# Decoder trunk on one core: weight loads by contraction halves in the ConvFFN's first two blocks, a large PSUM tile for their last product, another distribution of the adaLN sections, and merge tiles fetched ahead

## The chip, the cores and the metric

The kernel runs on one core of a Trainium2 chip, in one launch. The metric is the device time of the program in microseconds. The kernel before was run three times; its time is the median.

## The reference, cut to what matters

A residual trunk of two layers works on x (1024 tokens, 1024 channels, float32) and a conditioning vector c. Layer 0 has the even mixer (gated DeltaNet heads and pooling), layer 1 the odd mixer (dilated attention in three groups, merged per head). Behind each mixer stands a ConvFFN with 2816 hidden channels. In front of each of these four stands a norm with shift and scale from c, and a gate from c stands behind it.

```python
cs = jax.nn.silu(c)
for i in range(DEPTH):
    mod = (cs @ ada_w[i] + ada_b[i])[:, None, :]
    sh_m, sc_m, g_m, sh_f, sc_f, g_f = jnp.split(mod, 6, axis=-1)
    hm = rms_norm(x, norm_mix[i]) * (1.0 + sc_m) + sh_m
    ...
    x = x + g_m * y
    hf = rms_norm(x, norm_ffn[i]) * (1.0 + sc_f) + sh_f
    x = x + g_f * conv_ffn(hf, ffn_w_up[i], ffn_conv_w[i], ffn_conv_b[i], ffn_w_down[i])

def conv_ffn(h, w_up, conv_w, conv_b, w_down):
    up = h @ w_up
    gate, val = jnp.split(up, 2, axis=-1)
    gate = causal_dwconv(gate, conv_w) + conv_b
    return (jax.nn.silu(gate) * val) @ w_down
```

In the odd mixer each of the three attention groups gives an output and the logarithm of its softmax denominator per token and head; the outputs are added with weights that are the softmax of the three logarithms.

## The kernel before

**Layout and arithmetic.** Activations lie channel-major: eight tiles of 128 channels by 1024 tokens; a half is 512 tokens. A float32 product is made of three matmuls (`mm3`, L205 to L209): both operands are split into a high and a low part, and high by high, high by low and low by high are accumulated in PSUM. A product of one 128-column block with one half of the activations takes eight steps k of three matmuls each.

**Weights.** `granule` (L186 to L193) loads 128 x 512 floats into one of four raw buffers (`raw`), copies the high part on ScalarE into one of nine `whi` buffers and lets GpSimd subtract to get the low part into one of nine `wlo` buffers (`split`, L182). `unit_c` (L195) loads one column block of 128 output channels as two granules, contraction blocks k = 0 to 3 and k = 4 to 7. All loads are issued by SyncE.

**PSUM.** There are two large tiles (`mm_ps`, 128 x 1024) and four small ones (`s_ps`, 128 x 512). A tile that is asked for takes a buffer when its last reader has finished.

**Order.** The text of the program gives each instruction its rank. The tile framework places the buffers and decides the order on each engine; an instruction whose operands and buffer are there can be issued ahead of older ones. `weave` and `mix` set how the text of a chain of small steps is interleaved with a generator of dense products.

**Stages.** Even mixer (to about 510 us), its last projection woven with the next norm (`edge`), ConvFFN of layer 0 (about 554 to 1250), odd mixer (to about 2375), ConvFFN of layer 1, output.

**ConvFFN.** `first_two` (L1147 to L1169) computes channel blocks 0 and 1 directly: gate0 and val0 in the two large tiles, the first halves of gate1 and val1 in two small ones. For the first half of the tokens the four products run side by side, k by k (`units`, L212), interleaved with the norm of the second half; then gate0, val0, gate1 and val1 follow for the second half, one after the other (the last two in new small tiles). The projection ahead of it, `edge`, holds eight granules: four rows of weights, two granules each; it passes over the output blocks once for each half of the tokens. `conv_half` (L1118) does the depthwise convolution on ScalarE and VectorE, `act` (L1128) the silu and the product with val. From block 2 on, `up` (L1240) computes the two halves with seven products in place of eight (a11, a12, s2, s1, s3, s4, a22, four steps each), for which `h_sums` and `w_sums` form sums of activations and weights on VectorE. The products alternate between large and small PSUM tiles. Then the down stage (L1284 to L1288) applies pairs of hidden blocks, nine pairs, with `update` (L222): for each pair 16 output pieces (o, half), 2 x 3 matmuls each.

**adaLN sections.** `mod` is needed in 24 sections of 512 columns, 12 a layer. The first four are done at the start. The rest are generators (`ada_steps`, L259): a section is ten steps, namely the first load, eight multiply-adds (each with the load of the next 256 KB into a raw buffer), and a sum over partitions by TensorE transposes. The multiply-add is one VectorE instruction (L281) or, when `by_pool` is set, a ScalarE multiplication and a GpSimd addition (L275, L277). There are two accumulators. `step_back` is called once by every product step (L218), by `update` and by `up`; every `pace`-th call gives out one step, as long as fewer than `secs_due` sections are done. `sections(n)` gives out what is missing up to n at once. Before: pace 3 up to section 12 in the even mixer; pace 14 with 24 due in the up stage of layer 0, by VectorE; pace 2 in its down stage, by ScalarE and GpSimd, and the rest at its end.

**Merges.** After the attention of a head pair, `merge` (L1576) reads for each of eight token blocks the three groups' outputs (three DMAs of 128 x 2 x 130 floats into one of three `ld` buffers), forms the weights and adds; `turn_o` transposes the result. The DMAs of a block stand in the text right ahead of the instructions that read them.

Of the kernel before, what the change touches and what calls it, by code (L numbers as in the profile page):

```python
# [34 lines left out]
def trunk(ctx, tc, x, c, ada_w, ada_b, norm_mix, norm_ffn, ev_w_in, ev_w_out, gdn_conv_w,  # L35
# [69 lines left out]
    pa = [None]  # L105
    back = []
    by_pool = [False]
    beat, pace, secs_done, secs_due = [0], [3], [0], [12]

    def step_back(now=False):  # L110

# [75 lines left out]
    def granule(src, shape=None):  # L187
# [4 lines left out]
        split(hi, lo, raw, lo_eng[0])  # L192
        return hi, lo  # L193

    def unit_c(w, c0):  # L195

        blocks = []
        for g in range(0, KT, 4):
            hi, lo = granule(w[g * P:(g + 4) * P, c0:c0 + P].rearrange("(k p) c -> p k c", p=P),
                             ("p (k c) -> p k c", dict(k=4)))  # L200
            blocks += list(zip(blk4(hi), blk4(lo)))
        return blocks

    def mm3(ps, wb, mov, first, last):

# [244 lines left out]
    def even():  # L450
# [9 lines left out]
        with tc.tile_pool(name="pe", bufs=1) as pe:  # L460
# [266 lines left out]
            def dense():  # L727
# [9 lines left out]
                ready.add(("in", 0))  # L737
                back.append(ada_steps(0, range(16, 48, 4), raw_tile))
                back.append(ada_steps(1, range(0, 48, 4), raw_tile))
                with tc.issue_after(res["gt"].ins):  # L740
                    step_back(True)
                    step_back(True)
# [344 lines left out]
            drain(dn)  # L1087
            xt = res["x"]
            h2 = h_tiles()
            sections(12)  # L1090
            vec2 = norm_vec(0, 1)
            acc = edge(row_blocks(ev_w_out[0], (6, 7, 2, 3)), [*res["o67"], res[2], res[3]], gate, xt, vec2, h2, xs[2])
            return xt, h2, vec2, acc
# [2 lines left out]
    def ffn(l, xt, h, vec, acc, vec_next):  # L1096
        gate = mod[l][:, 40:48]
        wu, wd = ffn_w_up[l], ffn_w_down[l]
        with tc.tile_pool(name=f"pf{l}", bufs=1) as pf:
# [38 lines left out]
            def ext(dt=F32R, name="ext"):  # L1138
                return pf.tile([P, T], dt, tag="ext", name=nm(name), bufs=8)

            def wu_gate(j):
                return unit_c(wu, j * P)

            def wu_val(j):
                return unit_c(wu, DFF + j * P)

            def first_two():  # L1147

                gp, vp = mm_ps(), mm_ps()
                g, v = ([[p[:, s] for s in HS], [s_ps(), None]] for p in (gp, vp))  # L1150
                wb = [wu_gate(0), wu_val(0), wu_gate(1), wu_val(1)]
                t = [gate_tile(), gate_tile()]
                d = units([gp, vp, g[1], v[1]], wb, h, (0,))
                weave(norm(xt, vec, h, 1, acc, (4.5, 6.0), keep=True), d)
                drain(d)
                drain(units([gp], wb[:1], h, (1,)))
                for hf in range(2):
                    conv_half(t[0], g[0], 0, hf)
                conv_half(t[1], g[1], 1, 0)
                drain(units([vp], wb[1:2], h, (1,)))  # L1160
                act(t[0], v[0], 0)
                sums = h_sums()
                g[1][1] = s_ps()
                drain(units([[None, g[1][1]]], wb[2:3], h, (1,)))
                conv_half(t[1], g[1], 1, 1)
                v[1][1] = s_ps()
                drain(units([[None, v[1][1]]], wb[3:], h, (1,)))
                act(t[1], v[1], 1)
                return sums  # L1169
# [98 lines left out]
            sums = first_two()  # L1268
            a = w_sums(2)
            if l == 0:  # L1270
                secs_due[0], pace[0] = 24, 14
                with tc.issue_after(last_act[0].ins):
                    step_back(True)
                    step_back(True)
# [5 lines left out]
                up(j, b, a)  # L1280
                a = nxt
            xt = reload(xs[2 + l])
            pace[0], by_pool[0] = 2, True
            for j in range(0, NJ - 4, 2):  # L1284
                if j:
                    hid = [from_dram(hid_d[l][i]) for i in (j, j + 1)]
# [12 lines left out]
    def odd(xt, h, vec, acc):  # L1299
# [5 lines left out]
        with tc.tile_pool(name="po", bufs=1) as po:  # L1305
# [274 lines left out]
            def merge(hp, need):  # L1580
# [5 lines left out]
                elif hp == 3:  # L1586
                    o = [et("qkT", 4, (P, 2, T), F32R) for _ in range(2)]
                    o = [(t[:, 0, :], t[:, 1, :]) for t in o]
                    res["m3"] = [halves(*t) for t in o]
                mos = {}  # L1590

                def load(t):
                    ld = et("ld", 3, (P, 3, 2, 130))
                    for g in range(3):
                        nc.sync.dma_start(ld[:, g], osc[g][t * P:(t + 1) * P, hp * 2:hp * 2 + 2, :])
                    mx, e, dn = et("mx", 2, (P, 1, 2)), et("me", 2, (P, 3, 2)), et("dn", 2, (P, 3, 2))
                    nc.vector.tensor_reduce(out=mx[:, 0, :], in_=ld[:, :, :, 128].rearrange("p g x -> p x g"),
                                            axis=mybir.AxisListType.X, op=ALU.max)
                    nc.vector.tensor_tensor(out=e, in0=ld[:, :, :, 128], in1=mx.to_broadcast([P, 3, 2]), op=ALU.subtract)
                    nc.scalar.activation(e, e, AF.Exp)  # L1600
                    nc.vector.tensor_tensor(out=dn, in0=e, in1=ld[:, :, :, 129], op=ALU.mult)
                    nc.vector.tensor_reduce(out=mx[:, 0, :], in_=dn.rearrange("p g x -> p x g"),
                                            axis=mybir.AxisListType.X, op=ALU.add)
                    nc.vector.reciprocal(mx, mx)
                    nc.vector.tensor_tensor(out=e, in0=e, in1=mx.to_broadcast([P, 3, 2]), op=ALU.mult)
                    if t % 2 == 0:
                        mos[t // 2] = t2k()
                    for hh in range(2):
                        m = blk4(mos[t // 2])[hh * 2 + t % 2]
                        nc.scalar.activation(m, ld[:, 0, hh, 0:P], AF.Copy, scale=e[:, 0, hh:hh + 1])  # L1610
                        for g in (1, 2):
                            nc.vector.scalar_tensor_tensor(out=m, in0=ld[:, g, hh, 0:P], scalar=e[:, g, hh:hh + 1],
                                                           in1=m, op0=ALU.mult, op1=ALU.add)
# [127 lines left out]
```

## Time and profile before

| what | value |
|---|---|
| median of three runs | 3058.81 us (3058.46 to 3065.91) |
| the profiled execution | 3069.38 us, of which the span is 3067.3 us |
| mean granted TensorE clock in the span | 0.983 |
| HBM read / written | 251.82 / 77.00 MB |
| DMA packets of SyncE's and ScalarE's queue (q1) | 300.55 MB, 31.2% of 16 engines |

How to read it: PE is TensorE's matmuls, PEld its weight loads, DVE is VectorE, ACT ScalarE, POOL GpSimd, SP SyncE, whose DMA issues are not counted as busy. L207 is line 207 of the kernel. In a group, "sp<-hh,whi" is a matmul that writes a small PSUM tile from activations hh with weights whi; "mm" is a large one. "[1.65 <-ACT whi L184]" says that the engine was idle for 1.65 us before the instruction, and that the idle time ended with ScalarE's writing of whi on line 184. "x40: 733/752/1885" are 40 instructions with the shortest, the median and the longest duration in ns. Durations of matmuls overlap.

### The profile page before, as it was taken

Reading aid. Unit: us, or ns where it says so; the run is one execution under the profiler, and the core shown is the slowest. Engines: PE = TensorE matmul, PEld = TensorE weight load, DVE = VectorE, ACT = ScalarE, POOL = GpSimd, SP = SyncE. Lnnn points to the kernel's source line nnn. Section 1 sums busy time; section 2 is a strip of 40 time slices with the busy share of each in tenths; the row PEclk is TensorE's granted clock in tenths of the full one; section 3 lists DMA queues with packets and bytes.
Section 4 is the critical chain, followed back from the end, with each engine's and each line's share of the span. In section 5 each row is a group of like instructions: output and inputs, shape, how many; then the busy total and the mean of one; then the engine's idle time right before and its main releaser. Section 6 shows DMA issues by size and latency. Waiting matters only on the chain.

```text
span 3067.3 us, 40298 instructions
## 1 busy us (share of the span) xinstructions
PE 2965.9 (97%) x14346; PEld 2452.8 (80%) x14346; DVE 1945.1 (63%) x3781; ACT 1138.9 (37%) x2266; POOL 1033.0 (34%) x783
## 2 busy tenths in 40 slices
PE   6999999899999999999999999999999999999999
PEld 4777877778888887888888878888877788888888
DVE  6768745987776655654545646353687877776554
ACT  5433432533334433423333434333344433334210
POOL 4412323565556876200000010000032555556540
PEclk8999999999999999999999999999999999999999
DMA  7523314253323754322214242313253222224321
GB/s 247 142 61 107 96 59 151 72 155 110 110 86 102 237 156 138 129 67 73 92 62 123 72 145 74 106 41 113 65 175 117 73 89 83 83 83 168 110 91 58
DMA packets 275011, 331.47 MB, mean 108 GB/s; under 512 B 27411, under 2 KB 194426, under 8 KB 274810
## 3 DMA queue, kind: packets, MB, share of 16 engines
q1 hardware_dynamic: 266810, 300.55, 31.2%
q0 software_dynamic: 7040, 25.17, 2.4%
q10 hardware_dynamic: 960, 3.18, 0.3%
q8 instruction: 113, 1.85, 0.3%
q14 instruction: 88, 0.72, 0.1%
HBM read 251.82 MB, written 77.00 MB: 107 GB/s over the span
## 4 chain that ended last, share of the span: by engine, by line
PE 73%; DVE 6%; POOL 2%; issue 2%; DMA 2%; ACT 1%; SPq 0%; POOLq 0%; ACTq 0%; DVEq 0%
PE sp L209 11%; PE sp L207 11%; PE sp L208 11%; PE mm L1365 8%; PE mm L1363 8%; PE mm L1364 8%; PE mm L208 3%; PE mm L207 3%; PE mm L209 3%; PE sp L1559 2%; PE sp L1515 2%; PE sp L1395 1%; DVE xr L1181 1%; PE sp L1548 1%; POOL wlo L185 1%
## 5 line engine op out<-in xcount | busy, mean ns | idle before, releaser
L1363 PE MATMUL mm<-whi,hh 128*128 128x512 f32 x1152 | 482.6, 419 | 0.0
L1365 PE MATMUL mm<-whi,hl 128*128 128x512 f32 x1152 | 452.7, 393 | 0.0
L1364 PE MATMUL mm<-wlo,hh 128*128 128x512 f32 x1152 | 451.2, 392 | 0.0
L185 POOL TENSOR_TENSOR wlo<-raw,whi 128x512 fp32r<-128x512 f32 x190 | 250.0, 1331 | 492.6 <-ACT whi L184 425.0
L241 DVE SCALAR_TENSOR_TENSOR xr<-sp,mod,xr 128x512 f32<-128x512 f32 x336 | 251.1, 749 | 183.5 <-PE sp L209 183.5
L207 PE MATMUL sp<-oh,whi 128*128 128x512 f32 (+1 forms) x832 | 314.0, 377 | 1.6 <-ACT whi L184 1.6
L184 ACT ACTIVATE whi<-raw 128x512 fp32r<-128x512 f32 x334 | 207.9, 629 | 286.9 <-PE sp L208 100.9
L209 PE MATMUL sp<-oh,wlo 128*128 128x512 f32 (+1 forms) x832 | 311.7, 375 | 2.2 <-POOL wlo L185 1.9
L208 PE MATMUL sp<-ol,whi 128*128 128x512 f32 (+1 forms) x832 | 311.1, 374 | 0.0
L207 PE MATMUL mm<-hh,whi 128*128 128x512 f32 x704 | 285.3, 405 | 1.7 <-DVE big L609 1.7
L208 PE MATMUL mm<-hl,whi 128*128 128x512 f32 x704 | 280.0, 398 | 2.2 <-DVE hl L385 2.2
L185 POOL TENSOR_TENSOR wlo<-t2k,whi 128x512 fp32r<-128x512 f32 x160 | 228.3, 1440 | 156.2 <-ACT whi L184 96.8
L209 PE MATMUL mm<-hh,wlo 128*128 128x512 f32 x704 | 279.8, 397 | 0.0
L1460 POOL DMA_DIRECT2D vd<-v x24 | 17.6, 735 | 771.6 <-ACT v L1457 380.7
L1365 PEld LDWEIGHTS mm<-whi,hl 128*128 128x128 f32 x1152 | 216.4, 188 | 47.8
L1364 PEld LDWEIGHTS mm<-wlo,hh 128*128 128x128 f32 x1152 | 217.8, 189 | 37.0
L1363 PEld LDWEIGHTS mm<-whi,hh 128*128 128x128 f32 x1152 | 217.4, 189 | 36.0
L185 POOL TENSOR_TENSOR wlo<-wr,whi 128x512 fp32r<-128x512 f32 x114 | 179.2, 1574 | 159.5 <-ACT whi L184 151.4
L209 PEld LDWEIGHTS sp<-oh,wlo 128*128 128x128 f32 x832 | 157.2, 189 | 31.9 <-POOL wlo L185 4.2
L207 PEld LDWEIGHTS sp<-oh,whi 128*128 128x128 f32 x832 | 157.4, 189 | 29.8 <-ACT whi L184 2.5
L208 PEld LDWEIGHTS sp<-ol,whi 128*128 128x128 f32 x832 | 157.4, 189 | 26.9
L207 PE MATMUL sp<-hh,whi 128*128 128x512 f32 x384 | 152.3, 396 | 13.5 <-DVE ft L1107 10.2
(401 smaller groups left out, 6238.3 us busy)
## 6 DMA issues: line engine op xcount, KB each, us to landing
raw<-in_ada_w_dram SPq DMA_DIRECT2D x160, 256.0 KB
wr<-in_ffn_w_up_dram SPq DMA_DIRECT2D x76, 512.0 KB
raw<-in_od_w_in_dram SPq DMA_DIRECT2D x144, 256.0 KB
hid<-ft SPq DMA_DIRECT2D x44, 512.0 KB
raw<-in_ffn_w_down_dram SPq DMA_DIRECT2D x88, 256.0 KB
big<-hid SPq DMA_DIRECT2D x44, 512.0 KB
xr<-xs SPq DMA_DIRECT2D x32, 512.0 KB
os<-stg SPq DMA_DIRECT2D x96, 130.0 KB
```

The costliest lines, as they stand in the source:

```text
L184: nc.scalar.activation(dst_hi, src, AF.Copy)
L185: eng.tensor_tensor(out=dst_lo, in0=src, in1=dst_hi, op=ALU.subtract)
L207: nc.tensor.matmul(ps, wh, mh, start=first, stop=False)
L208: nc.tensor.matmul(ps, wh, ml, start=False, stop=False)
L209: nc.tensor.matmul(ps, wl, mh, start=False, stop=last)
L241: nc.vector.scalar_tensor_tensor(out=xt[o][:, s], in0=p, scalar=gate[:, o:o + 1], in1=xt[o][:, s], op0=ALU.mult, op1=ALU.add)
L1181: nc.vector.tensor_tensor(out=out, in0=x, in1=y, op=ALU.subtract)
L1363: nc.tensor.matmul(p, hh, wh, start=(k == 0), stop=False)
L1364: nc.tensor.matmul(p, hh, wl, start=False, stop=False)
L1365: nc.tensor.matmul(p, hl, wh, start=False, stop=(k == KT - 1))
L1515: nc.tensor.matmul(ps[:, at:at + len(ks) * P], qks[i][0][:, hh, blk * P:(blk + 1) * P], qks[i][1][:, hh, ks[0] * P:(blk + 1) * P], start=T ...
L1559: nc.tensor.matmul(ps[:, j * P:(j + 1) * P], pTs[n][:, a0 + c * P:a0 + (c + 1) * P], vb(kb, hh), start=(c == 0), stop=(c == len(ks) - 1))
```

## The change

1. `units_c` loads several column blocks by contraction halves: first the granule k = 0 to 3 of each column, then k = 4 to 7 of each. `first_two` uses it for its four columns. Before, each column was loaded whole, one after the other.
2. The last product of `first_two` (val1, second half) takes one half of a large PSUM tile instead of a small tile.
3. Sections: the even mixer does sections up to 10 at pace 4 (before: up to 12 at pace 3); the up stage of layer 0 up to 12 at pace 20 (before: up to 24 at pace 14); the down stage of layer 0 the other twelve, at pace 1, by ScalarE and GpSimd (before: what was left, at pace 2).
4. `merge` issues the DMAs of blocks t, t+1 and t+2 ahead of the work on block t.

```diff
-    beat, pace, secs_done, secs_due = [0], [3], [0], [12]
+    beat, pace, secs_done, secs_due = [0], [4], [0], [4]
...
+    def units_c(w, cols_):
+        blocks = [[] for _ in cols_]
+        for g in range(0, KT, 4):
+            for c0, b in zip(cols_, blocks):
+                hi, lo = granule(w[g * P:(g + 4) * P, c0:c0 + P].rearrange("(k p) c -> p k c", p=P),
+                                 ("p (k c) -> p k c", dict(k=4)))
+                b += list(zip(blk4(hi), blk4(lo)))
+        return blocks
+
     def unit_c(w, c0):
-        blocks = []
-        for g in range(0, KT, 4):
-            hi, lo = granule(w[g * P:(g + 4) * P, c0:c0 + P].rearrange("(k p) c -> p k c", p=P),
-                             ("p (k c) -> p k c", dict(k=4)))
-            blocks += list(zip(blk4(hi), blk4(lo)))
-        return blocks
+        return units_c(w, (c0,))[0]
...
                 back.append(ada_steps(1, range(0, 48, 4), raw_tile))
+                secs_due[0], pace[0] = 10, 4
...
-            sections(12)
+            sections(10)
             vec2 = norm_vec(0, 1)
...
-                wb = [wu_gate(0), wu_val(0), wu_gate(1), wu_val(1)]
+                wb = units_c(wu, (0, DFF, P, DFF + P))
...
-                v[1][1] = s_ps()
+                v[1][1] = mm_ps()[:, HS[0]]
                 drain(units([[None, v[1][1]]], wb[3:], h, (1,)))
...
             if l == 0:
-                secs_due[0], pace[0] = 24, 14
+                secs_due[0], pace[0] = 12, 20
...
             xt = reload(xs[2 + l])
-            pace[0], by_pool[0] = 2, True
+            if l == 0:
+                sections(12)
+                secs_due[0], pace[0], by_pool[0] = 24, 1, True
...
-                mos = {}
+                mos, lds = {}, {}
+
+                def fetch(t):
+                    lds[t] = et("ld", 3, (P, 3, 2, 130))
+                    for g in range(3):
+                        nc.sync.dma_start(lds[t][:, g], osc[g][t * P:(t + 1) * P, hp * 2:hp * 2 + 2, :])
 
                 def load(t):
-                    ld = et("ld", 3, (P, 3, 2, 130))
-                    for g in range(3):
-                        nc.sync.dma_start(ld[:, g], osc[g][t * P:(t + 1) * P, hp * 2:hp * 2 + 2, :])
+                    for t_ in range(t, min(t + 3, TT)):
+                        if t_ not in lds:
+                            fetch(t_)
+                    ld = lds[t]
```

More of the change, by code (lines that the diff above doesn't have):

```diff
@@ L1139, in ext @@
                 return pf.tile([P, T], dt, tag="ext", name=nm(name), bufs=8)
[L1141 to L1145, printed above, removed]
             def first_two():
```

## The prediction

> **What bounds the kernel now.** I read the page first, then the waits of TensorE, then its timeline around the longest of them, and last the windows of single stretches.
>
> ```profile
> span 3067.3 us, 40298 instructions
> ...
> PE 2965.9 (97%) x14346; PEld 2452.8 (80%) x14346; DVE 1945.1 (63%) x3781; ACT 1138.9 (37%) x2266; POOL 1033.0 (34%) x783
> ```
>
> TensorE is idle for 3067.3 - 2965.9 = 101 us; none of its matmuls is removed by the change, so the gain lies in those 101 us and in what follows an idle stretch. The profiled execution took 3069.4 us (the span and 2.1 us around it), 10.6 us above the median of 3058.8 of the runs. I make the sum as a difference against the profiled execution and carry the difference over to the median.
>
> In the waits of TensorE (total us, times, longest) two are of the kind that the change names:
>
> ```profile
> PE sp L207 <- DVE ft L1107: 10.2, 2, 6.5
> ...
> PE sp L1395 <- DVE t2k L1381: 5.4, 1, 5.4
> ```
>
> The first stands once in each ConvFFN, at the end of the first two channel blocks; the second is in a merge. The start of each ConvFFN has a pair of its own, here on TensorE's timeline (start, us, instruction, idle before it and its releaser), layer 0 and then layer 1:
>
> ```profile
> 558.50 0.50 PE L207 MATMUL sp<-hh,whi 128*128 128x512 f32 x1 [1.65 <-ACT whi L184]
> ...
> 561.98 0.79 PE L209 MATMUL sp<-hh,wlo 128*128 128x512 f32 x1 [2.52 <-POOL wlo L185]
> ...
> 2375.20 0.50 PE L207 MATMUL sp<-hh,whi 128*128 128x512 f32 x1 [1.64 <-ACT whi L184]
> ...
> 2378.68 0.80 PE L209 MATMUL sp<-hh,wlo 128*128 128x512 f32 x1 [2.52 <-POOL wlo L185]
> ```
>
> An idle stretch has a second price. In the windows below (stretch, its length, PE busy, PEld, DVE, ACT, POOL, granted clock, DMA share, GB/s) the clock is 0.50:
>
> ```profile
> 560.70:567.50 6.80, 5.52 (x15) 4.44 (x16) 3.87 (x3) 1.21 (x2) 4.61 (x4) 0.50 0.37 116
> 611.90:622.10 10.20, 5.85 (x14) 4.62 (x15) 10.20 (x14) 3.77 (x6) 6.39 (x5) 0.50 0.46 145
> 2376.60:2383.40 6.80, 4.71 (x13) 3.74 (x14) 3.57 (x3) 1.85 (x3) 5.41 (x4) 0.50 0.40 124
> ...
> 1205.80:1212.60 6.80, 5.63 (x13) 3.97 (x13) 1.64 (x3) 2.52 (x4) 3.39 (x3) 0.50 0.71 216
> ```
>
> Each lies at or right behind a wait. At half clock, half of the busy time is lost.
>
> **Weights by contraction halves: -13.4.** Before, the four columns are loaded one after the other, two granules each, so the first matmul of val1 (the fourth product at k=0) needs the seventh of eight granules. There are nine buffers for split weights; the projection ahead holds eight, four of which come free halfway through its second pass and four at its very end. The seventh granule is among the late ones: that is the pair of waits above. After the change the first matmuls need granules one to four, all in buffers that are free early. The second halves are needed at k=4, four times four products later. What goes: 1.65 + 2.52 and half of 5.52 = 6.9 in layer 0; 1.64 + 2.52 and half of 4.71 = 6.5 in layer 1. No instruction is added. What is late next would be the norm of the second half, but it shifts along, because VectorE waits there for TensorE:
>
> ```profile
> 567.08 0.69 DVE L313 TENSOR_REDUCE rs<-sp 128x4 f32<-128x512 f32 x1 [2.92 <-PE sp L312]
> ```
>
> The Trainium skill (TensorE: Matmul & The Clock Gate, "What's actually happening") has the clock halved after an idle window of about 3.4 us; the waits here are 1.65 and 2.52 us with matmuls between, and the windows still show 0.50, so the trace does not bear that threshold out for broken idle time. By the page the two half-clock terms would not belong to these waits and the part would bring 8.3.
>
> **The last small tile becomes a large one: -4, between -8.3 and +1.7.** There are four small PSUM tiles and two large ones. Now the last product (val1, second half) takes the fourth small one, and the second product of channel block 2 (a12) finds none: the 10.2 us of the wait above. Layer 0, in order of time:
>
> ```profile
> 601.44 0.39 PE L207 MATMUL sp<-hh,whi 128*128 128x512 f32 x1
> ...
> 604.90 0.20 DVE L1107 SCALAR_TENSOR_TENSOR ft<-mm,cols,ft 128x2 f32<-128x2 f32 x1
> ...
> 606.88 0.39 PE L207 MATMUL mm<-hh,whi 128*128 128x512 f32 x1
> ...
> 610.02 1.27 DVE L1132 TENSOR_TENSOR ft<-ft,mm 128x512 f32<-128x512 f32 x2
> ...
> 616.25 0.77 PE L207 MATMUL sp<-hh,whi 128*128 128x512 f32 x1 [6.49 <-DVE ft L1107]
> ...
> 621.51 0.63 PE L207 MATMUL sp<-ext,whi 128*128 128x512 f32 x1
> ```
>
> At 601.44 the last product starts, at 606.88 a11 (large), at 616.25 a12, at 621.51 the third product. Eight steps of three matmuls take 5.44 us, one 0.68. The change does not remove the scarcity, it moves it: the last product now needs gate0's large tile, free at 604.90 + 0.20 = 605.1 (a new wait of 3.7), and ends at 610.5; a11 then needs val0's large tile, free at 611.3, and ends at 614.0; a12 has a small tile at once and ends at 616.7. That is 4.8 earlier than 621.51. If the new wait halves the clock for 6.8 us, 3.4 of it are lost again. If a12 is put ahead of the last product, the third product waits for the small tile of 616.25: 5.3 earlier. Layer 1:
>
> ```profile
> 2417.79 0.39 PE L207 MATMUL sp<-hh,whi 128*128 128x512 f32 x1
> ...
> 2421.25 0.21 DVE L1107 SCALAR_TENSOR_TENSOR ft<-mm,cols,ft 128x2 f32<-128x2 f32 x1
> ...
> 2426.96 1.27 DVE L1132 TENSOR_TENSOR ft<-ft,mm 128x512 f32<-128x512 f32 x2
> ...
> 2429.83 0.47 PE L207 MATMUL sp<-hh,whi 128*128 128x512 f32 x1 [3.72 <-DVE ft L1107]
> ...
> 2433.92 0.63 PE L207 MATMUL sp<-ext,whi 128*128 128x512 f32 x1
> ```
>
> The same steps: tile free at 2421.5, end 2426.9, val0's tile 2428.2, a11 to 2431.0, a12 to 2433.7: 0.2 earlier, 3.1 later at half clock, 3.0 earlier with a12 put ahead. The sums are -5.0 as written, +1.7 with both half-clock stretches, -8.3 at best; I take -4, near the first. Behind the waiting product on TensorE stands all of block 2; VectorE waits only for val1's multiplication.
>
> **Sections dealt out anew: +1.** Of the 20 sections behind the first four, the even mixer did 8, now 6; the up stage of layer 0 did 4, now 2; the down stage did 8, now 12, by ScalarE and GpSimd.
>
> Even mixer, -2: two sections are 16 VectorE instructions of the row below, 12 us, fewer; and the others come later. Waits of TensorE there, on VectorE:
>
> ```profile
> L281 DVE SCALAR_TENSOR_TENSOR ada_acc<-raw,cs,ada_acc x56: 733/752/1885, 105.5 to 347.3; 128x512 f32<-128x512 f32 x56
> ```
> ```profile
> 148.79 1.11 PE L919 MATMUL sp<-ident,qkv 128*128 128x128 f32 x4 [3.70 <-DVE g L906]
> ...
> 168.98 1.09 PE L937 MATMUL sp<-ident,g 128*128 128x128 f32 x4 [3.47 <-DVE g L929]
> ```
>
> Both fall into the section steps' time. They are chains of a head's small instructions, of which section steps are only a part, so I take -2, between -7.2 (both go) and +3.7 (a section lands in another chain).
>
> Up stage, 0: TensorE was the bound (100 of 100 us busy):
>
> ```profile
> 700.00:800.00 100.00, 100.00 (x447) 82.84 (x446) 77.10 (x92) 35.61 (x51) 56.12 (x38) 1.00 0.33 106
> ```
>
> Down stage, +3. GpSimd's groups in 1000 to 1200 (busy, mean ns), then windows, then the waits at its end:
>
> ```profile
> L277 POOL TENSOR_TENSOR ada_acc<-ada_acc,raw 128x512 f32<-128x512 f32 x49 | 63.6, 1299 | 20.0 <-ACT ada_acc L275 12.0 <-ACT raw L275 6.1 <-POOL ada_acc L277 0.2
> L185 POOL TENSOR_TENSOR ol<-big,oh 128x1024 fp32r<-128x1024 f32 x20 | 48.0, 2401 | 12.7 <-ACT oh L184 12.5
> L185 POOL TENSOR_TENSOR wlo<-raw,whi 128x512 fp32r<-128x512 f32 x33 | 42.2, 1293 | 17.0 <-ACT whi L184 17.0
> ```
> ```profile
> 1000.00:1050.00 50.00, 50.00 (x225) 41.39 (x223) 30.81 (x43) 24.29 (x32) 40.96 (x27) 1.00 0.77 251
> ...
> 1014.00:1164.00 150.00, 150.00 (x675) 124.22 (x674) 87.67 (x120) 62.54 (x85) 119.73 (x81) 1.00 0.60 182
> ```
> ```profile
> 1202.88 0.50 PE L209 MATMUL sp<-oh,wlo 128*128 128x512 f32 x1 [1.22 <-POOL wlo L185]
> 1203.92 0.50 PE L207 MATMUL sp<-oh,whi 128*128 128x512 f32 x1 [0.54 <-ACT whi L184]
> 1205.34 0.50 PE L209 MATMUL sp<-oh,wlo 128*128 128x512 f32 x1 [0.69 <-POOL wlo L185]
> 1206.88 0.80 PE L207 MATMUL sp<-oh,whi 128*128 128x512 f32 x1 [1.04 <-ACT whi L184]
> ```
>
> A beat (one output block of one half, two products) is 2 x 0.68 = 1.36 us. With pace 1 a section of ten steps is due every 13.6 us, all twelve by beat 120 of 144. Two sections can be done ahead in the up stage (two accumulators), a third starts when the first is transposed, at about 1014. So from 1014 to beat 120 at 1163 GpSimd has ten sections of seven additions, 10 x 7 x 1.299 = 90.9, and the weights and hidden tiles of six pairs, 6 x (4 x 1.293 + 2 x 2.401) = 59.8: 151 us of work in 149, where it was busy for 119.7 before. It is full, but the last sections are not needed before the odd mixer's end and can slip into the last 24 beats. DMA: four sections more are 32 x 256 KB in 196 us, 43 GB/s on top of 182; the first row carried 251 without a wait. The load of one step stands on SyncE's queue among those of weights and hidden tiles, and all raw buffers (four) are released by GpSimd; a late section holds the next pair's weights back, and TensorE waits for those. Bounds: -6.3 if the sections end early and the four waits (3.5) with their half clock (half of 5.63) go; +34 if GpSimd can't exceed the 41.0/50 = 82% of the first row, 151/0.82 = 184 us. I take +3: the waits at the end stay and some are added.
>
> **Merges: 0, between -5.4 and +5.4.** Three buffers hold the fetched tiles, before and after. The instructions of an engine aren't issued in the order of the text here, and the fetches already run ahead:
>
> ```profile
> L1595 SPq DMA_DIRECT2D ld<-os x96: 319/424/822, 1415.4 to 2313.5; - x96
> ...
> L1597 DVE TENSOR_REDUCE mx<-ld x32: 147/162/165, 1672.0 to 2318.5; 128x2 f32<-128x6 f32 x32
> ```
>
> The first fetch is issued 257 us before the first read. A fetch waits for a buffer, and that isn't changed; the wait of 5.4 on L1395 bounds it either way.
>
> **Sum.** -13.4 - 4 - 2 + 0 + 3 + 0 = -16.4: 3053.0 for the profiled execution, 3042.4 against the median.
>
> **The rivals.** (1) GpSimd becomes the bound of layer 0's down stage: +34 in place of +3, 3042.4 + 31 = 3073. For it: 151 in 149, and 82% as the densest seen. Against: at 82% TensorE never waited, so it wasn't pushed. It decides from the point where the stage's loss exceeds the other terms' 19.4, which is 151/(149 + 19.4) = 90% of GpSimd's time. The Trainium skill (GPSIMD Engine Reference, "Engine selection") keeps element-wise additions off GpSimd, as about twice as slow as VectorE for two inputs; here it is 1299 against 752 ns, 1.7 times. (2) The gaps fill up again: of the first part only the plain waits go (8.3), the last small tile is even, the down stage costs 3: -5, 3053. For it: VectorE is busy for all of 611.90 to 622.10, so an earlier TensorE may meet the same late instructions. The case that the granules aren't issued in the new order, so that the first part does nothing, gives 3056 and belongs here. (3) All ends of the good side but the merges': -13.4 - 8.3 - 7.2 - 6.3 = -35, 3024.
>
> **How the numbers follow.** A measurement of this kernel can tell about 0.3%, 9.2 us: 3049.6 and 3068.0 are the edges. Forecast 0.49 (3030 to 3049), rival 1 0.15, rival 2 0.23, rival 3 0.13. Faster 0.49 + 0.13 = 0.62, same 0.23, slower 0.15. The range takes in the forecast, rival 2 and most of rival 3, and stops short of rival 1: 3022 to 3066.
>
> **What would show it.** Right: no wait of TensorE on whi and wlo at the start of either ConvFFN and clock 1.00 there; a wait of 3 to 4 us on L1107 moved to the last product of the first two blocks, or gone; GpSimd over 90% busy from 1014 to 1163; merges as before. Wrong: the pair of waits still there or as long further on, at k=4; waits of TensorE on wlo of over 19 us in the down stage; a merge that gains over 5.

## The result and the profile after

The changed kernel takes 3095.6 us (median of 4 runs, 3092.3 to 3097.8) against 3058.6 (4 runs, 3057.0 to 3065.9): ratio 1.0118, 95% interval 1.0105 to 1.0130. It is slower by 37 us, where 16 less were forecast. The spans of the profiled executions differ by 28.8 us (3096.1 and 3067.3); the one of before was 10.6 above its own median, and where these 10.6 lay turns out to matter below.

The stretches of the two traces, cut at the first matmul of each stage on TensorE's timeline:

| stretch (us) | before | after | difference |
|---|---|---|---|
| up to the first product of layer 0's ConvFFN | 554.7 | 550.9 | -3.7 |
| its first two channel blocks, to the third product of block 2 | 66.9 | 56.3 | -10.6 |
| the rest of the up stage | 378.4 | 380.6 | +2.2 |
| layer 0's down stage, to the odd mixer's first product | 253.0 | 296.8 | +43.9 |
| odd mixer, to the first product of layer 1's ConvFFN | 1118.5 | 1122.4 | +3.9 |
| first two blocks of layer 1 | 62.6 | 57.0 | -5.5 |
| the rest, to TensorE's last matmul | 628.9 | 627.5 | -1.4 |

The ends of the down stage stand in these rows (start, us, instruction), first of the kernel before:

```profile
999.88 0.39 PE L207 MATMUL sp<-oh,whi 128*128 128x512 f32 x1
...
1252.84 0.39 PE L1363 MATMUL mm<-whi,hh 128*128 128x512 f32 x1
```

and then of the changed kernel, in which the lines have moved by some (the matmuls of a product are L211 to L213, the section's multiplication and addition L279 and L281, the transposes L316):

```profile
987.79 0.39 PE L211 MATMUL sp<-oh,whi 128*128 128x512 f32 x1
...
1284.61 0.39 PE L1364 MATMUL mm<-whi,hh 128*128 128x512 f32 x1
```

The loss is there: 43.9 us, more than the 28.8 of the whole span. TensorE's waits between 985 and 1290 (total us, times, longest):

```profile
PE sp L213 <- POOL wlo L185: 14.3, 8, 3.7
PE sp L316 <- POOL ada_acc L281: 10.0, 2, 6.1
PE sp L212 <- POOL ol L185: 4.0, 1, 4.0
PE sp L211 <- ACT whi L184: 2.3, 3, 1.7
```

They make 30.6 us, where the prediction's rows have 3.5. Seven stretches of half clock stand behind them; the first, the last and the sum of a table of all seven (length, PE busy, ...):

```profile
1015.90:1019.30 3.40, 3.40 (x9) 2.63 (x8) 1.32 (x2) 1.78 (x2) 3.24 (x4) 0.50 0.68 218
...
1203.60:1210.40 6.80, 4.70 (x13) 3.89 (x14) 2.00 (x3) 2.37 (x4) 6.72 (x6) 0.50 0.55 154
sum 37.40, PE 32.65 PEld 24.58 DVE 12.74 ACT 18.27 POOL 32.66; mean PE 4.66 PEld 3.51 DVE 1.82 ACT 2.61 POOL 4.67
```

Half of the 32.65 is lost, 16.3. So 30.6 + 16.3 = 46.9 against 3.5 + 2.8 = 6.3 before: 40.6 of the 43.9. The prediction's window and GpSimd's three groups, from 1000 to 1200, answer to those of before:

```profile
1014.00:1164.00 150.00, 130.05 (x522) 102.49 (x523) 70.45 (x99) 73.55 (x100) 130.91 (x92) 0.90 0.66 198
```

```profile
L281 POOL TENSOR_TENSOR ada_acc<-ada_acc,raw 128x512 f32<-128x512 f32 x74 | 95.9, 1296 | 21.8 <-ACT ada_acc L279 13.9 <-ACT raw L279 4.2
L185 POOL TENSOR_TENSOR ol<-big,oh 128x1024 fp32r<-128x1024 f32 x19 | 45.5, 2398 | 4.3 <-ACT oh L184 4.2
L185 POOL TENSOR_TENSOR wlo<-raw,whi 128x512 fp32r<-128x512 f32 x28 | 35.2, 1282 | 0.6 <-ACT whi L184 0.5
```

25 additions more, five subtractions of weights fewer in the same time, and TensorE at 130 of 150 us where it was at 150. GpSimd is busy for 130.9, 87%. The loads of the sections on SyncE's queue show how many were left for the down stage:

```profile
641.22 0.33 SPq L269 DMA_DIRECT2D raw<-in_ada_w_dram  x1
968.30 3.86 SPq L269 DMA_DIRECT2D raw<-in_ada_w_dram  x3
975.47 4.20 SPq L269 DMA_DIRECT2D raw<-in_ada_w_dram  x4
```

The two sections of the up stage are loaded by 641. Then no section is loaded for 327 us, and all twelve remaining sections, with 84 additions, are loaded from 968 on. Six of the 84 begin ahead of the stage's first product at 987.79.

At the start of the ConvFFN the pair of waits on weights is gone, and others stand in its place; the granted clock is 0.50 there still, for 3.4 us in each layer (from 558.5 and from 2415.3). TensorE's waits over 0.25 us in the first two blocks of layer 1, after:

```profile
2414.99 0.79 PE L316 MATMUL sp<-ident,t2k 128*128 128x128 f32 x4 [3.06 <-DVE t2k L356]
2451.77 0.47 PE L211 MATMUL mm<-hh,whi 128*128 128x512 f32 x1 [0.29 <-DVE ft L1112]
2458.45 0.50 PE L211 MATMUL mm<-hh,whi 128*128 128x512 f32 x1 [0.96 <-DVE ft L1137]
2477.92 0.50 PE L211 MATMUL sp<-t,whi 128*128 128x512 f32 x1 [2.83 <-DVE ft L1252]
```

### The profile page after: what moved, and what is told of

It is laid out like the page before. It is cut to its first block, busy times and chain, and to the rows that moved or that the text cites. A ratio compares the mean times of both kernels' runs of the same rounds, so it can differ in the third digit from the quotient of the medians.

```text
span 3096.1 us, 40352 instructions
## 1 busy us (share of the span) xinstructions
PE 2974.9 (96%) x14346; PEld 2455.0 (79%) x14346; DVE 1917.1 (62%) x3749; ACT 1160.0 (37%) x2298; POOL 1071.2 (35%) x811
## 4 chain that ended last, share of the span: by engine, by line
PE 68%; DVE 6%; POOL 4%; DMA 3%; issue 3%; ACT 1%; SPq 0%; POOLq 0%; DVEq 0%; ACTq 0%
PE sp L213 10%; PE sp L211 10%; PE sp L212 10%; PE mm L1366 8%; PE mm L1364 8%; PE mm L1365 8%; PE mm L211 3%; PE mm L212 3%; PE mm L213 3%; POOL ada_acc L281 2%; PE sp L1560 2%; PE sp L1516 2%; PE sp L1396 1%; PE sp L1549 1%; POOL wlo L185 1%
## 5 line engine op out<-in xcount | busy, mean ns | idle before, releaser
L185 POOL TENSOR_TENSOR wlo<-raw,whi 128x512 fp32r<-128x512 f32 x190 | 258.8, 1378 | 500.5 <-ACT whi L184 417.2
L245 DVE SCALAR_TENSOR_TENSOR xr<-sp,mod,xr 128x512 f32<-128x512 f32 x336 | 251.6, 750 | 220.8 <-PE sp L213 220.0
L213 PE MATMUL sp<-oh,wlo 128*128 128x512 f32 (+1 forms) x832 | 317.2, 381 | 14.4 <-POOL wlo L185 14.3
L211 PE MATMUL sp<-oh,whi 128*128 128x512 f32 (+1 forms) x832 | 319.4, 384 | 2.3 <-ACT whi L184 2.3
L211 PE MATMUL mm<-hh,whi 128*128 128x512 f32 x720 | 292.2, 406 | 3.4 <-DVE big L613 1.5
L213 PE MATMUL mm<-hh,wlo 128*128 128x512 f32 x720 | 285.1, 396 | 0.0
L213 PEld LDWEIGHTS sp<-oh,wlo 128*128 128x128 f32 x832 | 159.9, 192 | 47.5 <-POOL wlo L185 18.9
L211 PEld LDWEIGHTS sp<-oh,whi 128*128 128x128 f32 x832 | 160.4, 193 | 31.9 <-ACT whi L184 3.9
L211 PEld LDWEIGHTS mm<-hh,whi 128*128 128x128 f32 x720 | 136.9, 190 | 32.4 <-DVE ft L1137 2.2
```

The source lines that it names most:

```text
L185: eng.tensor_tensor(out=dst_lo, in0=src, in1=dst_hi, op=ALU.subtract)
L211: nc.tensor.matmul(ps, wh, mh, start=first, stop=False)
L213: nc.tensor.matmul(ps, wl, mh, start=False, stop=last)
L245: nc.vector.scalar_tensor_tensor(out=xt[o][:, s], in0=p, scalar=gate[:, o:o + 1], in1=xt[o][:, s], op0=ALU.mult, op1=ALU.add)
```

## The experiments

All ratios are against the kernel before, measured beside each of them. "Stage" is the down stage of the one profiled execution, cut as above (253.0 before, 296.8 after).

**Each part alone.** Each kernel is the one before with one part of the diff above; `no_sections` is the changed kernel with the sections dealt as before.

sections_only: 

> The kernel before with the new distribution of the sections alone. Theory G (GpSimd is full in layer 0's down stage): the whole loss is here, 3058.6 + 44 in the down stage - 4 in the even mixer = about 3099. Rival I (the loss comes from the parts working together, since an earlier TensorE asks for the weights earlier): clearly less than that, 3060 to 3080.

halves_only: 

> The kernel before with loads by contraction halves alone. The prediction's sum: -13.4, so 3045, without the waits on whi and wlo at the start of both ConvFFNs. Rival (the gap fills up again at the second block's product a12): -5 or less, 3054 or more.

psum_only: 

> The kernel before with the large tile for the last product alone. The prediction's sum: -4, so 3055 (between 3050 and 3060), the wait of a12 on L1107 gone and a new one of 3 to 4 us in front of the last product. Rival (the order of the products changes so that the new wait does not arise): -8, 3050.

merges_only: 

> The kernel before with the merges' fetches ahead alone. The prediction: no change, within 3 us of 3058.6, the wait of about 5 us on L1382 or L1381 still there. Rival (SyncE issues the fetches in another order): the odd mixer 4 us longer, as in the trace of the changed kernel, or 5 shorter.

no_sections: 

> The changed kernel with the old distribution of the sections. Theory G: the gains of the two traces remain, 10.6 and 5.5 us at the starts of the two ConvFFNs, 2 of them given back in the up stage, so 3058.6 - 14 = about 3045, and the down stage is as before. Rival I: some of the down stage's waits stay, 3055 or more.

| kernel | us | before, us | ratio, 95% interval | stage |
|---|---|---|---|---|
| sections_only | 3101.8 | 3063.6 | 1.0131 [1.0115, 1.0148] | 295.2 |
| halves_only | 3062.8 | 3063.6 | 0.9996 [0.9982, 1.0011] | 254.8 |
| psum_only | 3064.3 | 3063.6 | 1.0003 [0.9992, 1.0015] | 254.1 |
| merges_only | 3056.8 | 3056.6 | 1.0004 [0.9994, 1.0014] | 252.3 |
| no_sections | 3060.2 | 3063.6 | 0.9991 [0.9978, 1.0003] | 249.9 |

The sections carry the whole loss. The other parts together are worth 0.1%, within the interval of nothing, where 17 us were forecast. So no_sections has the down stage that theory G expected, but not its total of 3045: the 10.6 and 5.5 us by which the starts of the two ConvFFNs are shorter in the traces are not found in the times.

**Which suspect in the down stage?** Four edits of the changed kernel; theory G says that GpSimd has too much to do, theory R that the shared raw buffers hold the weights up.

No additions (`no_adds` leaves the sections' seven additions out, so that their sums stay incomplete):

```diff
                 if by_pool[0]:
                     nc.scalar.activation(raw if k else acc, raw, AF.Copy, scale=cs[:, k:k + 1])
-                    if k:
-                        nc.gpsimd.tensor_tensor(out=acc, in0=acc, in1=raw, op=ALU.add)
```

> The changed kernel without the seven GpSimd additions of each section in layer 0's down stage (loads and ScalarE's multiplications stay; the sections' sums are left out). Theory G (GpSimd's time): the waits in the down stage go, about 3048. Rival R (the four raw buffers and the way of a load through them): a buffer is held for ScalarE only, 1.3 us less of some 5.5, so a part of the waits stays, 3065 to 3080.

Weights' low parts by VectorE in this stage (`lo_vector`):

```diff
                 secs_due[0], pace[0], by_pool[0] = 24, 1, True
+                lo_eng[0] = nc.vector
...
+            lo_eng[0] = nc.gpsimd
             js = range(NJ - 4, NJ)
```

> The changed kernel, but in layer 0's down stage VectorE subtracts for the weights' low parts (four of 1.29 us a pair leave GpSimd). Theory G: GpSimd has 47 us less over nine pairs, more than the stage lost, so about 3052. Rival R: the raw buffers are as scarce as before, 3080 to 3095.

Other buffers for the sections' loads, the eight of `t2k` (`own_buffers`):

```diff
-            raw = raw_of()
+            raw = t2k() if by_pool[0] else raw_of()
```

> The changed kernel, but the section loads of layer 0's down stage go to the eight t2k buffers, which are idle there, in place of the four raw ones. Theory G: GpSimd has as much to do, 3085 to 3098. Rival R: the weights no longer share their buffers, 3050 to 3065.

Four of the seven additions (`half_adds`: `if k:` becomes `if k % 2:`):

> The changed kernel with three of a section's seven GpSimd additions left out in layer 0's down stage (only those of the odd steps are made), so these sections' sums are not the reference's; loads, ScalarE products, transposes and their order stay. Theory G (GpSimd is full: its 101 us of additions, 48 of hidden tiles and 36 of weights between 988 and 1206 don't fit, and whatever is behind makes TensorE wait): 12 x 3 x 1.295 = 47 us of GpSimd's work go, more than the 44 of the loss, so the stage takes 252 to 256 us as with no additions at all, total 3049 to 3055. Theory O (the order: section steps stand ahead of the weights, and any addition in the chain delays them): four sevenths of the loss stay, the stage takes about 277, total 3073 to 3080.

| kernel | us | before, us | ratio, 95% interval | stage |
|---|---|---|---|---|
| no_adds | 3049.4 | 3056.6 | 0.9972 [0.9962, 0.9981] | 251.6 |
| lo_vector | 3098.9 | 3056.6 | 1.0141 [1.0126, 1.0156] | 299.9 |
| own_buffers | 3096.2 | 3056.6 | 1.0137 [1.0120, 1.0154] | 297.2 |
| half_adds | 3078.0 | 3062.1 | 1.0050 [1.0035, 1.0066] | 277.1 |

The additions are necessary for the loss: without them it is gone. This doesn't tell GpSimd's time from the order of the steps, since without additions the transposes need only a section's first multiplication. All loads and multiplications of the sections stay in no_adds, so they alone don't make the loss. R alone falls with own_buffers (3096.2, where it expected 3050 to 3065): TensorE no longer waits for weights, but now the sections' transposes wait, for just as long:

```profile
PE sp L316 <- POOL ada_acc L281: 34.1, 6, 13.5
PE sp L212 <- POOL ol L185: 3.9, 2, 3.5
```

In lo_vector GpSimd is rid of the weights' low parts (35.2 us in the rows of after), and the loss stays as well, above what either theory expected. VectorE's own queue takes over: its subtractions stand ahead of its updates of x. The last row is one of them: VectorE stands for 8.22 us at a subtraction whose weights are late, and the update behind it ends a wait of TensorE of 5.9 us.

```profile
PE sp L211 <- DVE xr L245: 25.6, 10, 5.9
PE sp L316 <- DVE xr L245: 8.8, 3, 5.2
```

```profile
1058.97 0.77 DVE L185 TENSOR_TENSOR wlo<-raw,whi 128x512 fp32r<-128x512 f32 x1 [8.22 <-ACT whi L184]
```

half_adds comes out as theory O had it (stage 277, total 3073 to 3080), and G as I had stated it falls. GpSimd here is less busy than before the change (107.3 of 150 us against 119.7), and TensorE loses time all the same:

```profile
1014.00:1164.00 150.00, 140.60 (x610) 113.59 (x609) 82.89 (x117) 78.06 (x109) 107.32 (x73) 0.96 0.68 217
```

```profile
PE sp L316 <- POOL ada_acc L281: 7.5, 2, 6.4
PE sp L213 <- POOL wlo L185: 5.9, 6, 1.3
PE sp L212 <- POOL ol L185: 3.2, 1, 3.2
PE sp L211 <- ACT whi L184: 3.0, 2, 2.7
```

With 0, 48 and 84 additions at this pace the stage takes 251.6, 277.1 and 296.8 us: about 0.53 us for each. Before the change 56 additions at half the pace cost nothing of the kind (253.0), so it isn't their number alone.

**Both at once.** half_own is half_adds with the edit of own_buffers.

> half_adds and own_buffers together: three of a section's seven GpSimd additions are left out in layer 0's down stage (so these sections' sums are not the reference's), and the section loads have buffers of their own in place of the four that they share with the weights. Theory B (two limits close together: GpSimd, asked for 9.1 us of additions per 13.6 us beside some 10 us of weights and hidden tiles per 21.8 us, and the four buffers, asked for ten loads per 13.6 us that each hold one for load, product and addition): with both relieved the stage takes 250 to 257 us, total 3047 to 3057. Theory O (the order of the steps: section steps stand ahead of the weights on every queue): the stage stays at 270 to 277, total 3070 to 3078.

3063.7 us against 3058.6, ratio 1.0019 [1.0009, 1.0029]; stage 268.2. The stage lies 2 us below O's range and 11 above B's, and the total between the two. The waits for weights are gone, and these are left:

```profile
PE sp L316 <- POOL ada_acc L281: 14.3, 3, 7.5
PE sp L212 <- POOL ol L185: 1.4, 1, 1.4
```

So with half the additions the shared buffers cost 8.9 us, and against no_adds 16.6 remain, mostly waits in which TensorE reaches the transposes of a section before its sum is there.

**Pace or number?** pace2 gives a step every second beat (`24, 1, True` becomes `24, 2, True`).

> The changed kernel with a section step every second beat of layer 0's down stage in place of every beat; seven of the twelve sections are then done within the stage and five in a row at its end, ahead of the products that need them. Theory G: the sum of GpSimd's work up to the odd mixer is the same, so the loss stays, only later: no wait on the weights' low parts in the stage, and 5 x 7 x 1.295 = 45 us of additions that TensorE waits for at the end, of which the last four blocks hide some 20: total 3080 to 3100. Theory P (the pace itself: a step every beat is more than the chain of load, product and addition can follow): the waits go with the pace, total 3055 to 3070.

3102.4 against 3062.1, ratio 1.0128 [1.0108, 1.0147]; stage 297.8. Course and size are those that theory G gave for this run, 2 us above its range, and theory P falls: within the stage TensorE loses next to nothing; then it stands still for five sections (two windows, and the wait):

```profile
1050.00:1189.00 139.00, 139.00 (x624) 115.14 (x624) 81.68 (x112) 53.27 (x74) 102.32 (x70) 1.00 0.52 160
1189.00:1240.00 51.00, 5.92 (x26) 3.94 (x25) 6.37 (x12) 24.17 (x35) 37.91 (x31) 0.54 0.60 175
```

```profile
PE sp L316 <- POOL ada_acc L281: 45.1, 5, 14.7
```

Of a section 9 us remain to be waited for even when little else runs, which are GpSimd's 7 x 1.296 = 9.1. At a step every second beat seven sections can be hidden, twelve cannot; at a step every beat all are given out in time, and the chain of load, multiplication and addition falls behind its place.

**Other distributions.** up6 puts six sections into the up stage and eight into the down stage, and keeps the even mixer's ten:

```diff
-                secs_due[0], pace[0] = 12, 20
+                secs_due[0], pace[0] = 16, 9
...
-                sections(12)
-                secs_due[0], pace[0], by_pool[0] = 24, 1, True
+                sections(16)
+                secs_due[0], pace[0], by_pool[0] = 24, 2, True
```

> The changed kernel with six sections in the up stage (to 16, a step every 9 beats, on VectorE) in place of two, and so eight in layer 0's down stage at a step every second beat, as before the change; the even mixer's share and the other three parts of the change stay. If the whole loss comes from the four sections more and the pace in the down stage, the stage takes 250 to 255 us and the total is 3055 to 3062. If the smaller share of the even mixer or the flush between the stages costs something too, 3063 or more.

3063.7 against 3062.1, ratio 1.0005 [0.9993, 1.0016]; stage 260.3, above the 250 to 255 that were expected, and the total just inside the second expectation. The kernel is where it was before the change, so most of the loss (36 of the 44 us of the stage) belongs to the number and the pace in the down stage. What the other 7 are was not tried. up8 goes the other way. It is no_sections with more sections in the up stage and fewer in the down stage:

```diff
-                secs_due[0], pace[0] = 24, 14
+                secs_due[0], pace[0] = 24, 8
...
-            pace[0], by_pool[0] = 2, True
+            pace[0], by_pool[0] = 3, True
```

> The three other parts of the change with the sections dealt as before in the even mixer (12), but eight of them in the up stage (a step every 8 beats, on VectorE) and only four in layer 0's down stage (a step every third beat). GpSimd has 4 x 7 x 1.295 = 36 us less to do there than before the change. If GpSimd's share alone decides, the four waits at the end of the stage (3.5 us) and their half clock go: total 3048 to 3055, against 3057 to 3060 before. If VectorE, 70 to 88% busy in the up stage, is the next bound, its 3 x 8 x 0.75 = 18 us more show as waits of the blocks' products there: 3058 to 3070.

3051.2 against 3062.1, ratio 0.9965 [0.9952, 0.9978]: faster than both kernels. By its additions (35 on GpSimd in the down stage, 56 before the change) it has five sections there and seven in the up stage, one less than planned. TensorE has no wait between 985 and 1240, the stage takes 243.2 us, and the up stage hides three sections more than before on VectorE: with the first two blocks it takes 442.3 us, 442.6 in no_sections.

**Why do the two parts at the ConvFFN's start gain nothing?** Both edits are made in up8, for the second half of the norm there (`moved`, called from `first_two`): up8_relief gives VectorE's four subtractions of the low parts to GpSimd, up8_vector gives GpSimd's four to VectorE.

```diff
-        (nc.vector if k % 2 else nc.gpsimd).tensor_tensor(
+        (nc.vector if k % 2 and not hl_pool[0] else nc.gpsimd).tensor_tensor(    # up8_relief
+        (nc.vector if k % 2 or hl_pool[0] else nc.gpsimd).tensor_tensor(         # up8_vector
```

up8_relief: 

> up8 with the four low-part subtractions that VectorE makes in the second half of the norm at each ConvFFN's start given to GpSimd. If VectorE's own instructions bound that stretch (35.0 of 35 us busy between 575 and 610 in up8), 4 x 0.68 = 2.7 us and more leave it in each layer, the stretch falls from 57.3 and 57.0 to 53 to 55, total 3045 to 3049. If GpSimd's instructions lengthen VectorE's beside them (the same subtraction takes 0.68 to 1.78 us on VectorE there, the long ones beside a GpSimd instruction of 1.3 to 1.7), the four come back as longer instructions: stretch 57 to 60, total 3051 to 3057.

up8_vector: 

> up8 with the other edit: the four low-part subtractions that GpSimd makes in the second half of that norm given to VectorE, so that VectorE makes all eight. If VectorE's own instructions bound the stretch, it grows by 4 x 0.68 = 2.7 us a layer, to about 60: total 3055 to 3058. If GpSimd's instructions cost VectorE about 1.1 us each, this gains 4 x (1.1 - 0.68) = 1.7 us a layer: stretch 55 to 56, total 3047 to 3050.

| kernel | us | before, us | ratio, 95% interval | first two blocks, layer 0 / 1 |
|---|---|---|---|---|
| up8 | 3051.2 | 3062.1 | 0.9965 [0.9952, 0.9978] | 57.3 / 57.0 |
| up8_relief | 3052.4 | 3058.6 | 0.9978 [0.9968, 0.9987] | 65.4 / 63.0 |
| up8_vector | 3046.1 | 3058.6 | 0.9958 [0.9943, 0.9973] | 54.9 / 55.3 |

With more work for VectorE and less for GpSimd the stretch is shorter by 2.4 and 1.8 us, as the second theory of up8_vector had it; in the reverse case it is longer by 8.2 and 6.0, more than either theory of up8_relief. VectorE, busy for 35.0 of 35 us from 575 to 610 in up8, bounds it, and GpSimd beside it makes VectorE slower (last section). Two things limit this reading. Each stretch is from one execution, and pace2, which has the changed kernel's code up to there, has 61.7 and 61.7 where the changed kernel has 56.3 and 57.0; the 2.4 and 1.8 us lie within such differences, the 8.2 and 6.0 beyond them. And in layer 0 the gap fills up again right behind the stretch, first up8, then up8_vector (up8_relief has no wait there):

```profile
624.15 0.80 PE L211 MATMUL sp<-t,whi 128*128 128x512 f32 x1 [3.12 <-DVE ft L1251]
```

```profile
625.84 0.80 PE L211 MATMUL sp<-t,whi 128*128 128x512 f32 x1 [6.17 <-DVE ft L1253]
```

From layer 0's first product to its down stage the three take 442.3 (up8), 442.8 (up8_vector) and 444.2 us (up8_relief), so little of this stretch reaches the total. up8_vector has the lowest ratio of all versions; up8's interval and its own overlap.

## Why the prediction was wrong

**The down stage, +3: the step that failed.** Measured +43.9. Two sentences of the prediction fell. "Two sections can be done ahead in the up stage": none was; the loads begin at 968, 20 us ahead of the stage. The steps are given out in the text only behind the up stage, and the two accumulators, free after the transposes at 704 and 840, did not bring them forward. So 11 additions lie ahead of 1014, where the prediction had 14, and 78 of the 84 behind the stage's first product. And "the last sections are not needed before the odd mixer's end and can slip into the last 24 beats": they can't. By the traces, where a step was given out, it has its place on SyncE's, ScalarE's, GpSimd's and TensorE's queues, ahead of the weights of later pairs, and when it is late they wait behind it: TensorE waits 10.0 us for sums of sections, though no product of the stage needs them, and 45.1 in pace2. The prediction named the other half itself ("a late section holds the next pair's weights back, and TensorE waits for those") and then priced it at next to nothing ("some are added"): the waits measured 30.6 us in place of 3.5, and the half clock behind them 16.3 in place of 2.8. own_buffers and lo_vector show the same time lost in three places, at the weights, the transposes or VectorE, according to whose queue is blocked. The upper bound of +34, taken from the densest window seen, was too low: it priced the stage's length by GpSimd's time and had no half clock in it.

**Rival 1 had the sign and the stage, not the mechanism.** It put the point of decision at GpSimd's being 90% busy. In the changed kernel it was 87%, in half_adds 72%, and both lost; before, at 80%, nothing was lost in the window. So GpSimd's share doesn't decide; how many steps are given out in how short a stretch does. The prediction's signs did not catch it either: the waits on wlo, 14.3 us, stayed under the 19 that were to show the forecast wrong. What exactly holds the last 16.6 us in half_own was not tried by itself and stays open. Its trace has four additions at 1170.1 and 1175.0, among GpSimd's subtractions of hidden tiles, ahead of the transposes that TensorE waits 7.52 us for.

**Weights by contraction halves, -13.4: the wait went, the time didn't.** halves_only has no wait on whi or wlo at the starts, as forecast. Measured against before it is 0.9996. The step at fault is "it shifts along, because VectorE waits there for TensorE": VectorE doesn't; it is late with the sum of squares ahead of the norm's transposes (the row of 3.06 above), and the next waits follow it. In layer 0 that sum ends 7.8 us after the ConvFFN's first product in both kernels, before (first row, 560.72 + 1.77 - 554.65) and after (558.77 - 550.92):

```profile
560.72 1.77 DVE L352 TENSOR_TENSOR t2k<-t2k,t2k 128x512 f32<-128x512 f32 x1 [0.70 <-ACT t2k L351]
```

```profile
557.00 1.77 DVE L356 TENSOR_TENSOR t2k<-t2k,t2k 128x512 f32<-128x512 f32 x1 [0.70 <-ACT t2k L355]
```

Before, TensorE was held up by the weights and came to the transposes later, at 565.99. In halves_only the waits of layer 0's start and of a12 are 3.11 + 6.74 = 9.9 us, where they were 1.65 + 2.52 + 6.49 = 10.7. In the executions of the kernel before and of merges_only, which has the same ConvFFN, the waits of layer 1's start make 1.64 + 2.52 + 3.72 + 2.28 = 10.2 us and, by the four rows of merges_only,

```profile
2361.34 0.50 PE L207 MATMUL sp<-hh,whi 128*128 128x512 f32 x1 [1.64 <-ACT whi L184]
2364.82 0.50 PE L209 MATMUL sp<-hh,wlo 128*128 128x512 f32 x1 [2.52 <-POOL wlo L185]
2411.96 0.47 PE L207 MATMUL sp<-hh,whi 128*128 128x512 f32 x1 [0.34 <-DVE ft L1107]
2429.74 0.50 PE L207 MATMUL sp<-t,whi 128*128 128x512 f32 x1 [3.88 <-DVE ft L1253]
```

8.4; after the change they make 7.1. That is the mechanism of rival 2, "the gaps fill up again". Its price of -8.3 for this part was still too much: the interval of halves_only reaches from about -5.5 to +3.4 us.

**The last small tile, -4.** In layer 0 its mechanism came out as drawn, in psum_only a wait of 3.62 in front of the last product where 3.7 was forecast (in layer 1 the same wait is only 0.29):

```profile
603.12 0.76 PE L207 MATMUL mm<-hh,whi 128*128 128x512 f32 x1 [3.62 <-DVE ft L1107]
```

and the stretch went from 66.9 to 63.0 and from 62.6 to 58.5. But the kernel's time is 1.0003 of that of before. The rows I costed belong to one execution: merges_only, with the same code there, takes 59.0 and 57.3 us for these stretches, 13 less than the profiled execution of before, whose total was 10.6 above the median; sections_only, also with that code, takes 58.2 and 57.9. The wait of 6.49 on L1107, the largest that I counted on, is 2.06 in merges_only and 0.36 in sections_only, but 6.74 in halves_only. These executions are no fair sample either: that of merges_only was the fastest of its ten, 5.5 under their median. So the wait differs that much from execution to execution, and I counted on the largest of one. That the saving came out of an excess that the median doesn't have is likely, and not shown.

**Even mixer, -2, and merges, 0.** The merges came out as said (1.0004). The first product of layer 0's ConvFFN lies between 545.2 and 554.7 us in the profiled executions; merges_only, with the old share of sections, has 549.2 and the changed kernel 550.9, so that no gain of the smaller share can be told.

## What to carry to other kernels

Background work that is dealt into a stage by a counter has to be priced by the queues on which each step gets its place, not by the sum of an engine's time: a step given out early and done late holds back everything behind it, and pace and number must both fit. Give such work to the stage and the engine that have room for it (three sections moved from GpSimd in the down stage to VectorE in the up stage: 0.9965 with the three other parts, which make 0.9991 by themselves), and before a wait is counted as a gain, look in a second execution whether it is there, and which engine is busy without a gap beside it.

## What the runs showed of the hardware

A VectorE subtraction of 128x512 floats with two SBUF operands takes 0.68 us, or up to 1.78 when GpSimd has begun one first. Rows of up8, GpSimd's and VectorE's:

```profile
580.22 0.68 DVE L1179 TENSOR_TENSOR xr<-xr 128x512 f32<-128x512 f32 x1
580.38 1.67 POOL L389 TENSOR_TENSOR hl<-xr,hh 128x512 fp32r<-128x512 f32 x1 [1.56 <-DVE hh L388]
580.82 1.78 DVE L389 TENSOR_TENSOR hl<-xr,hh 128x512 fp32r<-128x512 f32 x1
582.52 0.68 DVE L1179 TENSOR_TENSOR xr<-xr,xr 128x512 f32<-128x512 f32 x1
```

VectorE's instruction ends 0.55 us after GpSimd's, as if it had waited for that one's end. It goes the other way too: the next subtraction on GpSimd, begun while VectorE works off eight instructions of L1179 back to back, takes 5.85 us, where 1.29 is usual:

```profile
585.73 5.85 POOL L185 TENSOR_TENSOR wlo<-raw,whi 128x512 fp32r<-128x512 f32 x1 [3.68 <-ACT whi L184]
```

VectorE's groups from 575 to 610 show it as a mean. First the subtractions and the sums in up8, then the subtractions in up8_vector, where GpSimd has none of the eight, and the sums in up8_relief, where it has all:

```profile
L1179 DVE TENSOR_TENSOR xr<-xr 128x512 f32<-128x512 f32 x8 | 5.6, 717 | 0.0
L389 DVE TENSOR_TENSOR hl<-xr,hh 128x512 fp32r<-128x512 f32 x4 | 4.5, 1136 | 0.0
```

```profile
L389 DVE TENSOR_TENSOR hl<-xr,hh 128x512 fp32r<-128x512 f32 x8 | 5.3, 684 | 0.0
```

```profile
L1181 DVE TENSOR_TENSOR xr<-xr 128x512 f32<-128x512 f32 x8 | 9.1, 1181 | 0.0
```

Four subtractions cost VectorE 4.5 us, eight of them 5.3 when GpSimd keeps away; in up8_relief the sums on L1181 (L1179 in up8) rise from 717 to 1181 ns. The Trainium skill (SBUF — State Buffer, "SBUF: two separate sides") says that GpSimd and a VectorE instruction with two SBUF inputs take a shared port pair as an exclusive lock for the whole instruction; the trace agrees. VectorE's update of x on L245, with one operand in PSUM, takes 736 to 754 ns in all 336 cases of the changed kernel, those beside GpSimd's work in layer 0's down stage among them.
